# A recurrent mixer with its row modulation: the order of accumulations, gate products and the sum is changed, and rows and sums share one ring of buffers

## The chip, the core and the metric

The kernel runs on one core of a Trainium2 chip. The core has TensorE (matmuls, PE in the profile), VectorE (DVE), ScalarE (ACT), GpSimd (POOL) and SyncE (SP, whose queue issues the DMAs here). The metric is the device time of one execution in microseconds (us), the median of the runs.

## What is computed

One layer of a hybrid generator: a bidirectional gated linear recurrence (RG-LRU) over 256 context and 1024 latent tokens, with adaLN modulation, followed by a gated convolutional FFN. Cut to what the change touches:

```
sh1, sc1, g1, sh2, sc2, g2 = split((silu(c) @ mod_w + mod_b)[:, None, :], 6)   # rows of 1024
def lru_gates(xc, gate_w, gate_b, lam):                 # once for each direction
    pre = einsum("blhi,ghij->gblhj", xc.reshape(.., 10, 128), gate_w) + gate_b
    r, i = sigmoid(pre)
    log_a = -8 * softplus(-lam) * r
    return exp(log_a), sqrt(-expm1(2 * log_a)) * (i * xc)
def rglru_mixer(h, w_in, conv_w, conv_b, gates.., w_out):
    y, x = split(h @ w_in, 2)
    xc = dwconv1d(x, conv_w, conv_b)                    # 4 taps
    h_t = a_t * h_(t-1) + b_t                           # forwards and backwards
    return (gelu(y) * (h_fwd + h_bwd)) @ w_out
x = x + g1 * rglru_mixer(modulate(rms_norm(x), sh1, sc1))
x = x + g2 * conv_ffn(modulate(rms_norm(x), sh2, sc2))
```

## The kernel before

The 1280 channels of the recurrence are cut into ten blocks of 128, which lie across the partitions, with the 1280 tokens along the free dimension. Matrix products are made of three products of rounded parts: each operand is split into a high part (a cast on ScalarE, `S.copy`) and a low part (the difference, `lo_part`, on VectorE or GpSimd).

The loop `for t in range(NCH - 1)` (line 548) is what the text calls the passes, t = 0 to 8. In the code's own order, which the engines TensorE, VectorE, ScalarE and GpSimd keep, pass t does the following:

- TensorE runs the four gate products of block t (`gate(d, g)`, direction d, g = 0 for r and 1 for the input gate: three banks of 512, 512 and 256 tokens, nine matmuls), with the eight k steps of the next block's x product (`x_steps`) between them, then the two halves of the next block's y product (`y_half`). The gate products wait for `xs`, the split of the convolved x.
- ScalarE takes the sigmoids out of the banks (`gate_sig`), loads tables, makes the decays (`decay_a`, `decay_b`), the centre tap of the next convolution (`conv_centre`) and the casts.
- VectorE does the recurrence of the block before (`recur` for directions 0 and 1: r, b, then the scan), `gate_mul` for each input gate, the sum of both directions (`both`) and its product with the gelu (`gated`, which SP then stores), the other taps of the next convolution (`conv_taps`) and the low part of its split (`conv_split`).
- GpSimd makes the low parts of three weights in each pass: gate weights (`gwl`), and the x and y weights (`wl`).

Into this the kernel weaves the modulation rows g1, sh2, sc2, g2, eight halves of 512 columns. For each half, `mod_steps` has GpSimd clear an accumulator `macc` (one buffer), SP load the bias into its first row, and then eight times SP load 128 rows of the weight (`mraw`) and VectorE add them, scaled by silu(c), to `macc` (line 333). `mod(n)` takes n of these nine steps. When a half is full, `mod_hi` casts it to `mah`, `mod_lo` makes `mal`, `mod_sum` sums both over the partitions with a matmul against ones into a bank, and `mod_done` copies the bank to the row. The buffers of `mraw` are three, of `mah` and `mal` one each. The banks are five buffers of one pool (`bank()`); one that is asked for while all are taken waits for the reader of the one that comes free first.

Line 85 is `lo_part`, line 88 every matmul but the transposes (`mm`), line 439 `gate_mul`, lines 456 to 463 `recur`, 468 `both`, 472 `gated`, 405 `conv_taps`, 411 the casts of `conv_split`, 434 the sigmoids. SP's queue is not written by hand: its order is worked out when the program is built, and it is kept at run time.

Of the kernel before, what the change touches and what calls it, by code (L numbers as in the profile page):

```python
# [19 lines left out]
P = 128  # L20
# [22 lines left out]
XSPLIT = ((0, 512), (512, 1024), (1024, NTOK))  # L43
XLO_POOL = set()
HS_POOL = 0
MRAW = 3

GROUPS = tuple((j, j + 1) for j in range(0, NF, 2))
DOWN_LAST = {40: 3, 41: 1, 42: 2, 43: 3}
# [17 lines left out]
def tile_kernel(ctx: ExitStack, tc: tile.TileContext, x, cx, par, mod_b, mod1, mod2, wyx, gw, w_out, w_up, w_down, fw, out):  # L67
# [270 lines left out]
    def mod_hi():  # L338

        if not full:  # L340
            return None
        n, c, acc = full.pop(0)
        ah = mp.tile([P, 512], F32R, tag="mah", name="mah")
        al = mp.tile([P, 512], F32R, tag="mal", name="mal")
        S.copy(ah, acc)
        return n, c, acc, ah, al

    def mod_lo(m):
        if m:
            n, c, acc, ah, al = m  # L350
            lo_part(V, al, acc, ah)
# [10 lines left out]
    def mod_done(m):  # L362
        if not m:
            return
        n, c, pb = m
        dst = (g1, sh2, sc2, g2)[n]
        V.tensor_scalar(dst[:, c:c + 512], pb, float(n == 2), None, op0=ALU.add)
# [85 lines left out]
        return a  # L453

    def recur(d, a, r, b):
        V.scalar_tensor_tensor(r, a, 1.0, r, op0=ALU.add, op1=ALU.mult)  # L456
        V.tensor_tensor(b, b, r, op=ALU.mult)  # L457

        if d == 0:
            V.tensor_tensor_scan(a, a, b, 0.0, op0=ALU.mult, op1=ALU.add)  # L460
        else:
            V.tensor_tensor_scan(a[:, CTX - 1::-1], a[:, CTX - 1::-1], b[:, CTX - 1::-1], 0.0, op0=ALU.mult, op1=ALU.add)  # L462
            V.tensor_tensor_scan(a[:, NTOK - 1:CTX - 1:-1], a[:, NTOK - 1:CTX - 1:-1], b[:, NTOK - 1:CTX - 1:-1], a[:, 0:1], op0=ALU.mult, op1=ALU.add)  # L463
# [63 lines left out]
    with tc.manual_schedule(engines={ENG.PE, ENG.DVE, ENG.Activation, ENG.Pool}):  # L527
        xc = conv_centre(0, xp)
        wg = gate_weight(0)
        wx = weight(NCH + 1, G)  # L530
        conv_taps(0, xp, xc)
        xs = conv_split(xc)
        gy = y_done(y0)
        wy = weight(1, G)
        softplus_lambda()
        prev = None
        steps = mod_steps()

        def gate(d, g):
            bs = gate_mm(xs, wg, d, g)  # L540
            (r_t, b_t)[g][d] = dst = gate_sig(t, d, g, bs)
            return dst, bs

        def mod(n):
            for _ in range(n):
                next(steps, None)

        for t in range(NCH - 1):
            r_t, b_t = {}, {}
            xp, xo = x_outs()  # L550
            ks = iter(range(KD))

            def x_steps(n):
                for _ in range(n):
                    k_step(xo, CHUNKS, wx, next(ks))


            gate(0, 0)
            mh = mod_hi()
            x_steps(1)  # L560
            if prev:
                recur(0, prev[1][0], prev[2][0], prev[3][0])
            mod_lo(mh)
            i0 = gate(0, 1)
            if prev:
                recur(1, prev[1][1], prev[2][1], prev[3][1])
            gate_mul(*i0, xs[0])
            x_steps(2)
            pm = mod_sum(mh)
            mod(1)  # L570
            gate(1, 0)
            if prev:
                hs = both(prev[1], prev[2][1])
                gated(prev[0], hs, prev[4])
            mod_done(pm)
            x_steps(1)
            i1 = gate(1, 1)
            wg = gate_weight(t + 1)
            wx_next = weight(NCH + t + 2, G) if t < NCH - 2 else None
            mod(4)  # L580
            gate_mul(*i1, xs[0])
            x_steps(4)

            a_t = {d: wk.tile([P, NTOK], F32, tag="a", name="a", bufs=2) for d in range(2)}
            decay_a(t, 0, r_t[0], a_t[0])
            decay_b(t, 0, r_t[0])
            decay_a(t, 1, r_t[1], a_t[1])
            mod(4)
            xc = conv_centre(t + 1, xp)
            decay_b(t, 1, r_t[1])  # L590
            wy_next = weight(t + 2, G) if t < NCH - 2 else None
            conv_taps(t + 1, xp, xc)
            yb = [bank(), bank()]
            for q in range(2):
                y_half(yb, q, wy)
            wx, wy = wx_next, wy_next
            ordered(act(r_t[0], r_t[0], AF.Sqrt))
            xs = conv_split(xc)
            ordered(act(r_t[1], r_t[1], AF.Sqrt))
            prev = t, a_t, r_t, b_t, gy  # L600
            gy = y_done(yb)

        t = NCH - 1
        r_t, b_t = {}, {}
        gate(0, 0)
        recur(0, prev[1][0], prev[2][0], prev[3][0])
        i0 = gate(0, 1)
        gate_mul(*i0, xs[0])
        recur(1, prev[1][1], prev[2][1], prev[3][1])
        mh = mod_hi()  # L610
        mod_lo(mh)
        pm = mod_sum(mh)
        gate(1, 0)
        mod_done(pm)
        i1 = gate(1, 1)
        gate_mul(*i1, xs[0])
        hs = both(prev[1], prev[2][1])
        gated(prev[0], hs, prev[4])
        assert not full and next(steps, 0) == 0
# [290 lines left out]
```

## Time and profile before

| | us |
|---|---|
| median of 3 runs | 1323.93 |
| lowest and highest run | 1323.61, 1326.33 |
| the profiled execution | 1322.51 |
| its span, first to last instruction | 1320.7 |
| TensorE busy | 1243.8 (94%) |
| VectorE busy | 1052.8 (80%) |
| ScalarE busy | 548.7 (42%) |
| GpSimd busy | 426.3 (32%) |

A row of a timeline gives the start and the duration in us, the engine, the line, the operation, what it writes and reads with shapes, and how many equal ones are merged; in brackets stands the idle time ahead of it and what ended it. Matmuls are pipelined, so the distance between two starts tells more than a duration. A duration of VectorE or GpSimd holds what the instruction waited after it had begun.

### The profile page before, as it was taken

What the parts mean: (1) busy time and instruction counts of PE and PEld (TensorE: products, weight loads), DVE (VectorE), ACT (ScalarE), POOL (GpSimd) and SP (SyncE); (2) the same over time, 40 slices, a digit from 0 to 9 for tenths busy, and PEclk for the clock granted to TensorE, in tenths of its full rate; (3) what the DMA queues carried; (4) which work ended last, traced back from release to release, by engine and by line L of the source; (5) the groups of instructions that cost most, each with busy time, mean ns of one, the idle gap of its engine ahead of it and who ended that gap; (6) DMA issues with size and microseconds to landing.
All of it is one profiled execution on the core that took longest, in us unless ns stands there. A gap on an engine that the chain in (4) does not pass through costs nothing.

```text
span 1320.7 us, 14402 instructions
## 1 busy us (share of the span) xinstructions
PE 1243.8 (94%) x5512; PEld 1006.4 (76%) x5512; DVE 1052.8 (80%) x1193; ACT 548.7 (42%) x707; POOL 426.3 (32%) x238
## 2 busy tenths in 40 slices
PE   7789999898988889999999999999999999999995
PEld 6668777776767667878888888888888888888873
DVE  7968888888986877849977777777777777777788
ACT  6568776775777524433222222222222222222344
POOL 4632212111121300043143333333333333334565
PEclk8789999999998989999999999999999999999999
DMA  8413333332323464122111111111111111111003
GB/s 322 157 64 104 120 120 120 104 103 73 99 78 95 149 213 155 57 83 77 32 48 49 48 48 48 48 48 48 48 49 48 49 49 48 48 48 48 17 0 127
DMA packets 56740, 108.74 MB, mean 82 GB/s; under 512 B 4568, under 2 KB 24024, under 8 KB 56672
## 3 DMA queue, kind: packets, MB, share of 16 engines
q1 hardware_dynamic: 56528, 107.57, 24.5%
q8 instruction: 43, 0.70, 0.2%
q10 hardware_dynamic: 144, 0.26, 0.1%
q14 instruction: 25, 0.20, 0.0%
HBM read 98.37 MB, written 9.44 MB: 82 GB/s over the span
## 4 chain that ended last, share of the span: by engine, by line
PE 69%; DVE 18%; ACT 6%; DMA 3%; issue 3%; POOL 0%; SPq 0%; DVEq 0%; ACTq 0%
PE u L88 37%; PE pd L88 20%; PE pb L88 7%; PE xp L88 4%; DVE xc L405 3%; DMA mraw<-mod_dram 2%; DVE hl L213 2%; DVE a L463 2%; DVE macc L333 2%; DVE b L439 1%; DVE b L457 1%; DVE r L456 1%; DVE a L462 1%; ACT r L434 1%; DVE md L214 1%
## 5 line engine op out<-in xcount | busy, mean ns | idle before, releaser
L751 DVE SCALAR_TENSOR_TENSOR acc<-u,pr,acc 128x945 f32<-128x945 f32 (+2 forms) x352 | 427.0, 1219 | 23.3 <-ACT acc L744 15.9
L88 PE MATMUL u<-h2h,wl 128*128 128x512 f32 x704 | 277.7, 394 | 0.0
L88 PE MATMUL u<-h2l,wh 128*128 128x512 f32 x704 | 277.4, 394 | 0.0
L88 PE MATMUL u<-h2h,wh 128*128 128x512 f32 x704 | 274.4, 390 | 0.2 <-ACT h2h L717 0.2
L85 POOL TENSOR_TENSOR wl<-raw,wh 128x1024 fp32r<-128x1024 f32 x66 | 163.2, 2472 | 329.0 <-ACT wh L150 305.1
L784 DVE TENSOR_TENSOR x<-pd,x 128x512 f32<-128x512 f32 x160 | 109.6, 685 | 128.5 <-PE pd L88 128.5
L88 PEld LDWEIGHTS u<-h2l,wh 128*128 128x128 f32 x704 | 132.5, 188 | 31.7 <-DVE h2l L85 0.4
L88 PEld LDWEIGHTS u<-h2h,wh 128*128 128x128 f32 x704 | 132.5, 188 | 31.1 <-ACT h2h L717 0.5
L88 PEld LDWEIGHTS u<-h2h,wl 128*128 128x128 f32 x704 | 132.5, 188 | 28.1
L88 PE MATMUL pd<-dh,gl 128*128 128x512 f32 x320 | 126.3, 395 | 0.0
L88 PE MATMUL pd<-dl,gh 128*128 128x512 f32 x320 | 126.2, 394 | 0.0
L88 PE MATMUL pd<-dh,gh 128*128 128x512 f32 x320 | 125.2, 392 | 0.0
L830 ACT CAST gh<-acc 128x1024 fp32r<-128x1024 f32 x22 | 23.1, 1050 | 223.6 <-DVE acc L827 223.6
L85 POOL TENSOR_TENSOR gl<-acc,gh 128x1024 fp32r<-128x1024 f32 x18 | 43.2, 2400 | 199.0 <-ACT gh L830 199.0
L150 ACT CAST wh<-raw 128x1024 fp32r<-128x1024 f32 x64 | 67.2, 1050 | 79.4 <-PE u L88 73.4
L826 ACT ACTIVATE acc<-acc 128x1024 f32<-128x1024 f32 x22 | 23.3, 1060 | 182.8 <-DVE acc L751 182.8
L88 PE MATMUL xp<-hh,wh 128*128 128x512 f32 (+1 forms) x240 | 87.9, 378 | 1.9 <-ACT hh L223 1.9
L88 PE MATMUL xp<-hl,wh 128*128 128x512 f32 (+1 forms) x240 | 84.9, 378 | 4.0 <-POOL hl L85 4.0
L333 DVE SCALAR_TENSOR_TENSOR macc<-mraw,silu_c,macc 128x512 f32<-128x512 f32 x64 | 64.3, 1005 | 26.6 <-DMA mraw<-mod_dram 25.5
L88 PE MATMUL pb<-xh,gwh 128*128 128x512 f32 (+1 forms) x120 | 46.5, 387 | 27.1 <-DVE b L439 11.5
L88 PEld LDWEIGHTS pd<-dh,gl 128*128 128x128 f32 x320 | 60.0, 187 | 13.9
L88 PEld LDWEIGHTS pd<-dh,gh 128*128 128x128 f32 x320 | 60.1, 188 | 13.7
(188 smaller groups left out, 2306.6 us busy)
## 6 DMA issues: line engine op xcount, KB each, us to landing
raw<-w_up_dram SPq DMA_DIRECT2D x44, 512.0 KB, 3.6
mraw<-mod_dram SPq DMA_DIRECT2D x64, 256.0 KB, 3.5
raw<-wyx_dram SPq DMA_DIRECT2D x20, 512.0 KB, 3.5
dr<-w_down_dram SPq DMA_DIRECT2D x40, 256.0 KB, 3.8
ld<-mod_dram SPq DMA_DIRECT2D x16, 512.0 KB, 5.1
rgr<-rgd SPq DMA_DIRECT2D x16, 512.0 KB, 4.0
rgd<-r SPq DMA_DIRECT2D x10, 512.0 KB, 2.7
wor<-w_out_dram SPq DMA_DIRECT2D x10, 512.0 KB, 4.6
```

Source lines behind the costliest of these rows:

```text
L85: eng.tensor_tensor(lo, src, hi.bitcast(F32), op=ALU.subtract)
L88: T.matmul(o, w, r, start=start, stop=stop)
L150: S.copy(wh, raw)
L213: V.scalar_tensor_tensor(hl[KD - 1][:, :D], mr[k][s], 1.0, row, op0=ALU.mult, op1=ALU.mult, accum_out=md1[:, k, s, v:v + 1])
L214: V.tensor_scalar(md1[:, k, s], md1[:, k, s], mod_b1(k, s), None, op0=ALU.add)
L333: V.scalar_tensor_tensor(acc, r, silu_c[:, kk, 0:1], acc, op0=ALU.mult, op1=ALU.add)
L405: V.scalar_tensor_tensor(xc[:, oa:ob], xp[:, oa + s:ob + s], pr[:, C_CW + t * 4 + tap:C_CW + t * 4 + tap + 1], xc[:, oa:ob], op0=ALU.mult, ...
L463: V.tensor_tensor_scan(a[:, NTOK - 1:CTX - 1:-1], a[:, NTOK - 1:CTX - 1:-1], b[:, NTOK - 1:CTX - 1:-1], a[:, 0:1], op0=ALU.mult, op1=ALU.add)
L751: V.scalar_tensor_tensor(o, uv[:, r0 + dy:r1 + dy, c0 + dx:c1 + dx], w(dy, dx), o, op0=ALU.mult, op1=ALU.add)
L784: V.tensor_tensor(xs, pd, xs, op=ALU.add)
L826: ordered(act(aa, aa, AF.Silu))
L830: S.copy(gh, aa)
```

## The change

`mah` and `mal` are taken from the ring of `mraw` (tag "mraw"), which grows from three to five buffers. `recur` is cut into `recur_in` (r and b) and `recur_scan`. In the passes the second direction's scan moves behind the first `gate_mul`; one accumulation goes between the directions, two behind `gated`, four stay ahead of the taps and one goes between the taps and the split; the cast, low part, matmuls and copy of the sum move to later places of the pass. In the last block, t = 9, the calls for a sum, of which none is left there, are dropped.

```
-MRAW = 3
+MRAW = 5
...
-        ah = mp.tile([P, 512], F32R, tag="mah", name="mah")
-        al = mp.tile([P, 512], F32R, tag="mal", name="mal")
+        ah = mp.tile([P, 512], F32R, tag="mraw", name="mah", bufs=MRAW)
+        al = mp.tile([P, 512], F32R, tag="mraw", name="mal", bufs=MRAW)
...
     def recur(d, a, r, b):
+        recur_in(a, r, b)
+        recur_scan(d, a, b)
+
+    def recur_in(a, r, b):
         V.scalar_tensor_tensor(r, a, 1.0, r, op0=ALU.add, op1=ALU.mult)
         V.tensor_tensor(b, b, r, op=ALU.mult)
+
+    def recur_scan(d, a, b):
...
             gate(0, 0)
-            mh = mod_hi()
             x_steps(1)
             if prev:
-                recur(0, prev[1][0], prev[2][0], prev[3][0])
-            mod_lo(mh)
+                recur_in(prev[1][0], prev[2][0], prev[3][0])
+                recur_scan(0, prev[1][0], prev[3][0])
+                mod(1)
             i0 = gate(0, 1)
+            mh = mod_hi()
             if prev:
-                recur(1, prev[1][1], prev[2][1], prev[3][1])
+                recur_in(prev[1][1], prev[2][1], prev[3][1])
             gate_mul(*i0, xs[0])
             x_steps(2)
-            pm = mod_sum(mh)
-            mod(1)
             gate(1, 0)
+            if prev:
+                recur_scan(1, prev[1][1], prev[3][1])
+            mod_lo(mh)
             if prev:
                 hs = both(prev[1], prev[2][1])
                 gated(prev[0], hs, prev[4])
-            mod_done(pm)
             x_steps(1)
             i1 = gate(1, 1)
+            pm = mod_sum(mh)
+            mod(3)
             wg = gate_weight(t + 1)
             wx_next = weight(NCH + t + 2, G) if t < NCH - 2 else None
-            mod(4)
             gate_mul(*i1, xs[0])
+            mod_done(pm)
             x_steps(4)
...
             ordered(act(r_t[0], r_t[0], AF.Sqrt))
+            mod(1)
             xs = conv_split(xc)
...
-        mh = mod_hi()
-        mod_lo(mh)
-        pm = mod_sum(mh)
         gate(1, 0)
-        mod_done(pm)
         i1 = gate(1, 1)
```

What this does to VectorE's row of instructions in a pass, from the split of the convolution to the next taps. Before:

```order
L85 TENSOR_TENSOR mal<-macc,mah 128x512
L456 SCALAR_TENSOR_TENSOR r<-a,r 128x1280
L457 TENSOR_TENSOR b<-b,r 128x1280
L462 SCALAR_TENSOR_TENSOR a<-a,b 128x256
L463 SCALAR_TENSOR_TENSOR a<-a,b 128x1024
L439 TENSOR_TENSOR b<-pb,xc 128x512 x2
L439 TENSOR_TENSOR b<-pb,xc 128x256
L468 TENSOR_TENSOR r<-a 128x1024
L472 TENSOR_TENSOR r<-r,gy 128x1024
L367 TENSOR_SCALAR g_80<-pb 128x512
L333 SCALAR_TENSOR_TENSOR macc<-mraw,silu_c,macc 128x512 x4
```

VectorE now, the same stretch, from the accumulation that follows the scan of direction 0:

```order
L333 SCALAR_TENSOR_TENSOR macc<-mraw,silu_c,macc 128x512
L460 SCALAR_TENSOR_TENSOR r<-a,r 128x1280
L461 TENSOR_TENSOR b<-b,r 128x1280
L439 TENSOR_TENSOR b<-pb,xc 128x512 x2
L439 TENSOR_TENSOR b<-pb,xc 128x256
L468 SCALAR_TENSOR_TENSOR a<-a,b 128x256
L469 SCALAR_TENSOR_TENSOR a<-a,b 128x1024
L85 TENSOR_TENSOR mal<-macc,mah 128x512
L474 TENSOR_TENSOR r<-a 128x1024
L478 TENSOR_TENSOR r<-r,gy 128x1024
L333 SCALAR_TENSOR_TENSOR macc<-mraw,silu_c,macc 128x512 x2
```

The product b of the first input gate stands ahead of the two scans of direction 1, the low part of the sum behind them, and the accumulations are spread. (`a<-a,b` are the scans.)

On SP's queue the rows of a pass stood like this before, from the bias to the y weights (`DMAHW` are the DMA queues' own semaphores, the others name the engine that is waited for):

```order
L328 DMA macc<-mod_b_dram 1x512 [waits Pool_49]
L473 DMA rgd<-r 128x1024 [waits DVE_49]
L332 DMA mraw<-mod_dram 128x512 [waits DMAHW7_49,DMAHW5_49,DVE_49]
L332 DMA mraw<-mod_dram 128x512 [waits DMAHW0_49,DVE_49]
L332 DMA mraw<-mod_dram 128x512 [waits DMAHW1_49,DVE_49]
L156 DMA raw<-wyx_dram 128x1024 [waits Pool_49]
```

And on SP now:

```order
L328 DMA macc<-mod_b_dram 1x512 [waits Pool_49]
L332 DMA mraw<-mod_dram 128x512 [waits DMAHW5_49]
L479 DMA rgd<-r 128x1024 [waits DVE_49]
L332 DMA mraw<-mod_dram 128x512 [waits PE_49]
L332 DMA mraw<-mod_dram 128x512 [waits DMAHW6_49,DMAHW0_49,DVE_49]
L332 DMA mraw<-mod_dram 128x512 [waits DMAHW7_49,PE_49]
L156 DMA raw<-wyx_dram 128x1024 [waits Pool_49]
```

One row's load now stands ahead of the store of the gated product (`rgd<-r`), and two of the three behind it wait for TensorE, whose sum reads the buffers that they take.

## Rows read from the trace of the kernel before

**Rows 1.** The page's chain that ended last: share of the span by line.

```profile
PE u L88 37%; PE pd L88 20%; PE pb L88 7%; PE xp L88 4%; DVE xc L405 3%; DMA mraw<-mod_dram 2%; DVE hl L213 2%; DVE a L463 2%; DVE macc L333 2%; DVE b L439 1%; DVE b L457 1%; DVE r L456 1%; DVE a L462 1%; ACT r L434 1%; DVE md L214 1%
```

**Rows 2.** Busy time by pass (stretch, us, engines, PEclk, DMA): passes 1, 8, sum.

```profile
122.08:155.96 33.88, 33.10 (x160) 26.99 (x158) 28.45 (x31) 23.52 (x30) 7.64 (x4) 1.00 0.36 117
...
381.12:422.85 41.73, 37.47 (x159) 30.23 (x159) 30.49 (x31) 29.83 (x37) 7.05 (x3) 0.88 0.23 72
sum 300.77, PE 276.60 PEld 222.16 DVE 254.66 ACT 210.57 POOL 57.24; mean PE 34.58 PEld 27.77 DVE 31.83 ACT 26.32 POOL 7.15
```

**Rows 3.** Timeline of TensorE in pass 1: first matmuls of blocks.

```profile
130.86 0.39 PE L88 MATMUL pb<-mah,ones_r 128*128 128x512 f32 x1
...
131.32 0.39 PE L88 MATMUL pb<-xh,gwh 128*128 128x512 f32 x1
...
134.21 0.40 PE L88 MATMUL xp<-hh,wh 128*128 128x512 f32 x1
...
135.96 0.39 PE L88 MATMUL pb<-xh,gwh 128*128 128x512 f32 x1
...
137.69 0.40 PE L88 MATMUL xp<-hh,wh 128*128 128x512 f32 x1
```

**Rows 4.** Timeline of TensorE in pass 4: third bank of gate(1, 0).

```profile
245.78 0.38 PE L88 MATMUL pb<-xh,gwh 128*128 128x256 f32 x1 [1.78 <-DVE b L439]
```

**Rows 5.** Timeline of VectorE in pass 1.

```profile
119.98 1.48 DVE L456 SCALAR_TENSOR_TENSOR r<-a,r 128x1280 f32<-128x1280 f32 x1
...
123.03 2.82 DVE L460 TENSOR_TENSOR_SCAN a<-a,b 128x1280 f32<-128x1280 f32 x1
126.37 0.69 DVE L85 TENSOR_TENSOR mal<-macc,mah 128x512 fp32r<-128x512 f32 x1 [0.52 <-ACT mah L345]
...
130.03 0.69 DVE L462 TENSOR_TENSOR_SCAN a<-a,b 128x256 f32<-128x256 f32 x1
...
133.02 1.60 DVE L439 TENSOR_TENSOR b<-pb,xc 128x512 f32<-128x512 f32 x3
134.53 1.22 DVE L468 TENSOR_TENSOR r<-a 128x1024 f32<-128x1024 f32 x1
...
136.93 0.68 DVE L367 TENSOR_SCALAR g<-pb 128x512 f32<-128x512 f32 x1
137.53 2.32 DVE L333 SCALAR_TENSOR_TENSOR macc<-mraw,silu_c,macc 128x512 f32<-128x512 f32 x3
...
149.80 4.83 DVE L405 SCALAR_TENSOR_TENSOR xc<-xp,pr,xc 128x254 f32<-128x254 f32 x6
155.37 1.63 DVE L85 TENSOR_TENSOR xl<-xc,xh 128x512 fp32r<-128x512 f32 x3 [0.74 <-ACT xh L411]
```

**Rows 6.** Timelines of GpSimd and VectorE where the two meet.

```profile
106.57 2.87 POOL L85 TENSOR_TENSOR wl<-raw,wh 128x1024 fp32r<-128x1024 f32 x1
...
139.19 1.80 POOL L85 TENSOR_TENSOR gwl<-raw,gwh 128x512 fp32r<-128x512 f32 x1 [11.54 <-ACT gwh L381]
...
254.03 2.86 POOL L85 TENSOR_TENSOR wl<-raw,wh 128x1024 fp32r<-128x1024 f32 x1
...
391.47 3.33 POOL L85 TENSOR_TENSOR wol<-wor,woh 128x1024 fp32r<-128x1024 f32 x1 [16.39 <-ACT woh L482]
...
106.00 5.66 DVE L333 SCALAR_TENSOR_TENSOR macc<-mraw,silu_c,macc 128x512 f32<-128x512 f32 x4
...
254.54 1.61 DVE L439 TENSOR_TENSOR b<-pb,xc 128x512 f32<-128x512 f32 x3
```

**Rows 7.** SP's bias issue, DMA in 0.5 us behind it, landing of `mraw` loads.

```profile
200.57 0.24 SPq L328 DMA_DIRECT2D macc<-mod_b_dram  x1
...
201.00:201.50 0.50, 0.50 (x4) 0.45 (x3) 0.47 (x2) 0.00 (x0) 0.00 (x0) 1.00 0.03 4
...
DMA to landing us min/median/max: 2.7/3.5/3.7
```

**Rows 8.** Timeline of ScalarE in pass 1: the centre tap.

```profile
145.53 1.43 ACT L397 ACTIVATE xc<-xp,pr 128x1280 f32<-128x1280 f32 x1
```

## The prediction

> **What bounds the kernel now.** I read the chain of work that ended last first. It is TensorE's for the most part, but beside the matmuls it lists VectorE's accumulations of the row modulation (2% of the span) and the loads that these wait for (2% more) [rows 1]. Both belong to the mixer loop, so the second view is the busy table by pass of that loop, each stretch running from the first gate matmul of a pass to that of the next. Passes 1 to 8 take 300.77 us together, pass 1 33.88 and pass 8 41.73, with 160 and 159 matmul records; the granted clock is 1.00 in pass 1 and 0.88 in pass 8 [rows 2]. So matmul work does not set the time of a pass; waits do, and what the clock loses behind them.
>
> What would a pass take without waits? Pass 1 has one block that is too long: the gate block from 131.32 to 134.21 takes 2.89 where the next such block, 135.96 to 137.69, takes 1.73 [rows 3]. 33.88 less the 1.16 between them is **32.72 us**. Eight of these are 261.8, so some 39.0 us lie in these passes for any change of this kind.
>
> Whom TensorE waits for is seen in pass 4: 1.78 us for the product b of VectorE [rows 4], because the third bank of gate(1, 0) is freed by `gate_mul` of the first gate, and that stands behind both scans of direction 1.
>
> **The change, step by step.** Every pass keeps its matmuls, its eight accumulations, its GpSimd operations and its bytes. What moves is the order on VectorE, TensorE's sum and SP's queue, and with them the waits. I lay out pass 1 anew in the printed times: TensorE begins at 122.08 (the start of the stretch in [rows 2]), VectorE at 119.98, 2.10 us ahead [rows 5].
>
> *TensorE.* The two sum matmuls (0.46, 130.86 to 131.32 [rows 3]) move behind gate(1, 1). Without them and without the wait the block of gate(1, 1) begins 1.62 earlier, at 134.34, and the pass ends at 122.08 + 32.72 = 154.80.
>
> *VectorE*, by the distances between starts in [rows 5]; a step's successor begins 0.09 before the printed end (133.02 + 1.60 against 134.53), so an accumulation, three of which take 2.32, counts about 0.76 in a row and 0.67 alone. r and b of direction 0, 3.05, and its scan, 2.82: 125.85. The moved accumulation, 0.67: 126.52; the wait of 0.52 for the cast of the sum, which stood here, is gone. r and b of direction 1, 3.05: 129.57. `gate_mul`, 1.51: 131.08. Its first third is over by 130.1, and TensorE comes to that bank at 134.34 - 1.75 - 0.35 = 132.2 (one x step and a third of a block earlier), so a wait as in pass 4 is covered by 2 us. The scans of direction 1, 2.99: 134.07. The low part of the sum, 0.69 less that 0.09, 0.60: 134.67; TensorE reads it at 134.34 + 1.73 = 136.07, so the new wait in front of its x matmuls is covered by 1.4. The sum of the directions and its product, 2.40: 137.07. Then two accumulations (1.45), the second `gate_mul` (1.5), the sum's copy (0.60), four accumulations (3.03), taps with the 0.74 behind them (5.57) and the split (1.55). The last accumulation stands in those 0.74, in which VectorE waits for ScalarE's cast anyway, so 0.67 costs nothing; without that cover it would cost 0.67 a pass. All of it: 3.05 + 2.82 + 0.67 + 3.05 + 1.51 + 2.99 + 0.60 + 2.40 + 1.45 + 1.5 + 0.60 + 3.03 + 5.57 + 1.55 = 30.8 us without waits.
>
> *GpSimd* brings the waits. The low part of the gate weights is asked for 3.23 after the block of gate(1, 1) begins (135.96 [rows 3] to 139.19 [rows 6]), now at 137.57. That is inside the first accumulation (137.07 to about 137.8). How the two engines collide is seen at 106.57: a GpSimd operation that came during the first of four accumulations ran next, and the four took 5.66 instead of 3.1 [rows 6]. So the second accumulation waits out the gate weights, 1.3 us, and the third waits for what is left of the next operation, 2.4 us. Between these two accumulations lie the product and the copy, 2.1 us, which read PSUM; a product at 254.54 took its usual 1.61 in the middle of a GpSimd operation that began at 254.03 [rows 6]. So 0.3 is left. Bounds: nothing if GpSimd comes after both accumulations, 1.3 + 2.4 = 3.7 if it comes before 137.07. I take 1.6, the case of the layout, whose margin is 0.5 us. VectorE's pass is then 32.4 against TensorE's 32.72, so its lead and that margin grow from pass to pass.
>
> *Loads.* Two of five buffers' uses in each turn are now the sum's parts. So two of the rows for the four accumulations wait for TensorE's sum, and all three that are not yet loaded stand on SP's queue behind the store of the gated product, which waits until 137.07. SP issues them at about 137.5 to 138.5; a row lands 2.7 to 3.7 later [rows 7], by 142.2. VectorE wants the last at 144.6: covered by 2.4. The next weights, behind these on SP, have ten us to spare. The new start of a sum also waits for its bias row: GpSimd clears the sum behind the low part (I set 0.6 for its 512 columns, as VectorE's copy of as many takes), then SP issues. In pass 3 this was at 200.57 and the row moved before 201.50 [rows 7]; with the same again for its semaphore I take 1.1 us. 134.67 + 0.6 + 1.1 = 136.4, ahead of 137.07. Bounds: that, and the 3.7 of a whole row, 1.9 a pass late. The Trainium skill's page "DMA: Bandwidth & Descriptors", section "Anatomy of one DMA", gives about 2.0 us of fixed cost per transfer for its GpSimd path; this load goes by SP and the trace shows less, and by the page it would land at 137.3 and cost an estimated 0.2 a pass.
>
> *ScalarE.* The centre tap began 6.34 after the gate weights were asked for (139.19 to 145.53 [rows 6, 8]); so now at 143.9, ending at 145.3, where VectorE's accumulations end at 145.4. No wait.
>
> Passes 1 to 7 take 32.72. *Pass 8* has one accumulation left, and a GpSimd operation for the output weights, which takes 3.33 today [rows 6]. Its cast now stands ahead of the first sigmoids, so it meets the first scan: VectorE is 2.4 late, and its lead hides half. I take 1.2 (bounds 0 and 3.3): 33.9.
>
> Sum: 7 x 32.72 + 33.9 = 262.9 against 300.77, **37.9 us saved**. What follows is TensorE's matmuls as before and shifts along. The profiled execution took 1322.51, so 1284.6; the median of the runs lies 1.42 above it: **1286 us**.
>
> **The rivals.** *GpSimd takes its whole price (B).* If its operation comes 0.5 earlier against VectorE, the product and the next accumulation wait 1.3 and 2.4, VectorE's pass is 30.8 + 3.7 = 34.5, its lead is gone, TensorE then follows it through `gate_mul`, and every further pass is alike. Pass 1 at 33, six at 34.5, pass 8 at 36: 276, saved 24.8, 1299; if it starts only later in the loop, between 1286 and 1299. For it: the margin is small. Against it: VectorE's pass is the shorter one without it. The Trainium skill's page "SBUF — State Buffer", section "SBUF: two separate sides", says that VectorE operations with two SBUF inputs and GpSimd take one port pair as an exclusive lock, and that the loser blocks for the whole instruction. By that rule accumulations put beside GpSimd's work are paid in full, which is this rival's 34.5; the trace agrees that they block (5.66 for 3.1).
>
> *A third collision (C).* If in B the four accumulations run later still, the low part of the y weights, which meets the taps otherwise (they read PSUM), meets them, 2.4 more: six passes at 36.9, with 33 and 36: 290, saved 10.4, 1314. For it: that low part follows the centre tap closely, and the tap ends where the accumulations end. Against it: a late VectorE delays the centre tap as well, since the tap's buffer is read by the second `gate_mul`.
>
> *The loads become the wait (D, the slower one).* The last three rows are issued only behind the gated product. They are wanted 6 us after that. Each us beyond holds seven passes, so all is given back from 6 + 37.9/7 = 11.4 us to landing; at 12.5 it is 1331. The longest landing is 3.7 [rows 7].
>
> *The wait only changes its name (E).* If ScalarE's sigmoids hold TensorE wherever VectorE did, nothing is saved: 1324.
>
> **How the numbers follow.** Forecast 0.50; B, whole or from a later pass, 0.34; C 0.08; D 0.04; E 0.04. The range 1281 to 1304 holds the first two (0.84): B is up to 5 us worse if pass 8 and the bias row are at their upper bounds too, and the low end is eight passes at 32.72 (1285) less some us of the last pass, whose wait I don't price. Faster by over 0.2% (about what a measurement here can tell from no change) 0.92, within it 0.04, slower 0.04.
>
> **What the profile will show.** Passes 1 to 7 at 32.7, clock 1.00, no wait for b: right. Passes of 34 to 35 with the gated product or an accumulation drawn out by 1.3 and 2.4 beside GpSimd: B. Accumulations that wait for loads: D. Waits for r at the gates in each pass: E. I am wrong at the root if the loop shrinks and the total does not.

## The result and the profile after

| | before | changed |
|---|---|---|
| median (us) | 1324.49 | 1284.08 |
| lowest and highest of 4 runs | 1323.61, 1326.33 | 1282.26, 1291.12 |
| the profiled execution | 1322.51 | 1282.26 |
| its span | 1320.7 | 1280.5 |
| TensorE busy | 1243.8 (94%) | 1227.7 (96%) |
| VectorE busy | 1052.8 (80%) | 1045.2 (82%) |

The changed kernel takes 0.9703 of the time before (95% interval 0.9665 to 0.9741), 40.4 us less. In the profiled executions the span is 40.2 shorter: 39.31 of it in passes 1 to 8, 0.34 ahead of them (the loop's pass 1 begins at 121.74 where it began at 122.08), and 0.55 behind them (1280.5 - 383.20 against 1320.7 - 422.85). The 0.34 and 0.55 are no more than executions of one kernel differ by: in another execution of the changed kernel ("changed, again" below) the passes take 261.46 as well, but begin at 123.45. One of the four runs took 1291.12; four more runs of the same kernel lie between 1283.24 and 1284.86.

The busy table by pass answers to [rows 2]. Columns: stretch, its length, then busy time and count for TensorE, its weight loads, VectorE, ScalarE, GpSimd, the granted clock, DMA share and GB/s.

```profile
121.74:154.40 32.66, 32.66 (x159) 27.14 (x158) 31.64 (x35) 26.77 (x33) 7.06 (x4) 1.00 0.36 122
...
317.70:350.36 32.66, 32.66 (x159) 27.14 (x158) 31.54 (x35) 26.57 (x32) 6.95 (x4) 1.00 0.33 106
350.36:383.20 32.84, 32.84 (x160) 27.13 (x159) 26.97 (x28) 26.18 (x32) 8.58 (x3) 1.00 0.29 91
sum 261.46, PE 261.46 PEld 217.07 DVE 247.87 ACT 212.43 POOL 57.40; mean PE 32.68 PEld 27.13 DVE 30.98 ACT 26.55 POOL 7.17
```

TensorE is busy for the whole of each pass: 32.66 of 32.66, seven times over, and 261.46 of 261.46 in all. The clock is 1.00 throughout, where pass 8 had 0.88. No row of TensorE in these passes has a wait of its own left, neither for b [rows 4] nor for r.

VectorE in pass 1, and GpSimd beside it, answer to [rows 5, 6]:

```profile
125.46 0.73 DVE L333 SCALAR_TENSOR_TENSOR macc<-mraw,silu_c,macc 128x512 f32<-128x512 f32 x1
...
129.03 1.61 DVE L439 TENSOR_TENSOR b<-pb,xc 128x512 f32<-128x512 f32 x3
130.56 0.68 DVE L468 TENSOR_TENSOR_SCAN a<-a,b 128x256 f32<-128x256 f32 x1
...
133.54 0.67 DVE L85 TENSOR_TENSOR mal<-macc,mah 128x512 fp32r<-128x512 f32 x1
...
136.52 2.54 DVE L333 SCALAR_TENSOR_TENSOR macc<-mraw,silu_c,macc 128x512 f32<-128x512 f32 x2
138.99 1.60 DVE L439 TENSOR_TENSOR b<-pb,xc 128x512 f32<-128x512 f32 x3
140.51 0.67 DVE L367 TENSOR_SCALAR g<-pb 128x512 f32<-128x512 f32 x1
141.11 3.15 DVE L333 SCALAR_TENSOR_TENSOR macc<-mraw,silu_c,macc 128x512 f32<-128x512 f32 x4
144.86 4.83 DVE L405 SCALAR_TENSOR_TENSOR xc<-xp,pr,xc 128x254 f32<-128x254 f32 x6 [0.60 <-ACT xc L397]
149.61 0.74 DVE L333 SCALAR_TENSOR_TENSOR macc<-mraw,silu_c,macc 128x512 f32<-128x512 f32 x1
...
137.21 1.30 POOL L85 TENSOR_TENSOR gwl<-raw,gwh 128x512 fp32r<-128x512 f32 x1 [2.42 <-ACT gwh L381]
138.46 2.87 POOL L85 TENSOR_TENSOR wl<-raw,wh 128x1024 fp32r<-128x1024 f32 x1
```

GpSimd's request comes at 137.21, 0.69 behind the start of the first accumulation. The two accumulations take 2.54; the same two took 1.53 in pass 6, where the request came a little later. So the collision costs 1.0 here. The product at 138.99 takes its usual 1.60 beside GpSimd. In passes 2 to 7 the request comes 1.0 behind the first accumulation, and the collision moves to the group of four behind the product, which loses 1.3 there. Pass 2, VectorE:

```profile
172.41 4.39 DVE L333 SCALAR_TENSOR_TENSOR macc<-mraw,silu_c,macc 128x512 f32<-128x512 f32 x4
```

Two rows of the waits by engine and line, of all eight passes (who waits for whom, us in total, times, longest), of the changed kernel:

```profile
DVE xc L405 <- ACT xc L397: 8.7, 8, 5.0
DVE macc L333 <- DMA mraw<-mod_dram: 1.2, 3, 0.5
```

And the same view of the kernel before, in a row that the prediction did not show:

```profile
DVE macc L333 <- DMA mraw<-mod_dram: 24.2, 19, 2.4
```

The accumulations' waits for loads fell from 24.2 us to 1.2. A row lands later than before (median 4.4 after issue against 3.5), yet it is there when it is wanted.

### The profile page after: what moved, and what is told of

Read it like the earlier page. It is cut to its first block, busy times and chain, and to the rows that moved or that the text cites. A ratio compares the mean times of both kernels' runs of the same rounds, so it can differ in the third digit from the quotient of the medians.

```text
span 1280.5 us, 14366 instructions
## 1 busy us (share of the span) xinstructions
PE 1227.7 (96%) x5512; PEld 1000.2 (78%) x5512; DVE 1045.2 (82%) x1193; ACT 550.6 (43%) x707; POOL 426.6 (33%) x238
## 4 chain that ended last, share of the span: by engine, by line
PE 83%; DVE 11%; ACT 3%; issue 2%; DMA 1%; POOL 0%; SPq 0%; DVEq 0%; ACTq 0%
PE u L88 38%; PE pd L88 20%; PE pb L88 14%; PE xp L88 10%; DVE hl L213 2%; DVE xc L405 1%; DVE md L214 1%; DVE stat L112 1%; DMA ld<-x_dram 1%; DVE rgl L85 1%; PE pt L720 0%; DVE x L790 0%; DVE b L461 0%; PE pb L270 0%; DVE o L860 0%
## 5 line engine op out<-in xcount | busy, mean ns | idle before, releaser
L88 PE MATMUL xp<-hh,wh 128*128 128x512 f32 (+1 forms) x240 | 84.9, 366 | 1.8 <-ACT hh L223 1.8
L88 PE MATMUL xp<-hl,wh 128*128 128x512 f32 (+1 forms) x240 | 82.0, 366 | 4.4 <-POOL hl L85 3.7
L88 PEld LDWEIGHTS pd<-dh,gh 128*128 128x128 f32 x320 | 60.1, 188 | 13.7
L88 PEld LDWEIGHTS pd<-dl,gh 128*128 128x128 f32 x320 | 60.0, 187 | 13.6
L769 POOL TENSOR_TENSOR dr<-dr,g 128x512 f32<-128x512 f32 x40 | 52.0, 1318 | 53.8 <-DMA dr<-w_down_dram 53.8
```

The source lines that it names most:

```text
L88: T.matmul(o, w, r, start=start, stop=stop)
L769: G.tensor_tensor(raw, raw, g2[:, cs], op=ALU.mult)
```

## The experiments

The passes now stand at TensorE's own time. What the runs had to settle is which part brings this, and whether the margins were as the prediction put them. Three theories were set against each other. **Turn**: a pass lasts the longer of TensorE's 32.66 and VectorE's own turn, and a VectorE that comes late meets GpSimd and becomes later still. **Product**: TensorE's waits for b, and the clock lost behind them, are the matter, so the early product brings the gain. **Loads**: the 24.2 us are the matter, so the ring brings it.

| kernel | eight passes | median | ratio to before (95%) |
|---|---|---|---|
| before | 300.77 | 1324.49 | 1 |
| changed | 261.46 | 1284.08 | 0.9703 (0.9665 to 0.9741) |
| ring alone | 274.47 | 1296.36 | 0.9794 (0.9755 to 0.9832) |
| product alone | 306.55 | 1329.34 | 1.0045 (1.0027 to 1.0064) |
| ring and product | 274.42 | 1298.04 | 0.9821 (0.9804 to 0.9837) |
| changed, no ring | 289.75 | 1313.66 | 0.9924 (0.9895 to 0.9953) |
| changed, product late | 271.29 | 1294.03 | 0.9768 (0.9732 to 0.9805) |
| changed, accumulations together | 275.11 | 1297.28 | 0.9826 (0.9796 to 0.9857) |
| changed, three accumulations early | 276.27 | 1298.60 | 0.9832 (0.9801 to 0.9863) |
| changed, four buffers | 261.48 | 1283.44 | 0.9720 (0.9683 to 0.9757) |
| changed, sum early | 261.55 | 1283.80 | 0.9724 (0.9694 to 0.9753) |
| changed, last block reordered | 261.46 | 1282.93 | 0.9707 (0.9690 to 0.9724) |
| changed, again | 261.46 | 1283.87 | 0.9715 (0.9699 to 0.9730) |

Each ratio is to runs of the kernel before that were taken with it (medians 1320.67 to 1324.49), so medians of different rows compare to a few us only; the eight passes of the profiled executions compare better.

**The ring alone**, on the kernel before:

```
-MRAW = 3
+MRAW = 5
...
-        ah = mp.tile([P, 512], F32R, tag="mah", name="mah")
-        al = mp.tile([P, 512], F32R, tag="mal", name="mal")
+        ah = mp.tile([P, 512], F32R, tag="mraw", name="mah", bufs=MRAW)
+        al = mp.tile([P, 512], F32R, tag="mraw", name="mal", bufs=MRAW)
```

> The kernel before with one part of the change: rows and sums share five buffers; every other order as before. Three theories. Turn: a pass lasts as long as the longer of TensorE's 32.66 and VectorE's own turn, which in the kernel before was lengthened by waits for loads (24.2 us in the eight passes), by the wait for the sum's cast (0.5 a pass) and by GpSimd's collisions. Then the ring takes away the 3.0 of loads a pass, and the turn is 30.8 + 0.67 (the accumulation that is not hidden) + 0.5 + some 2.2 of collisions = 34.2: eight passes 274, time about 1297 (1293 to 1305). Loads: the 24.2 us are the whole matter, so the ring alone brings nearly all: below 1290. Product: the waits of 1.78 and 3.26 for b, and the clock lost behind them, are the matter; the ring leaves them: 1315 or more, and waits for b in passes 2, 4, 6, 8 as before.

Measured: 1296.36, the turn theory's number, but not by its mechanism. Seven passes are alike at 33.80 to 33.88, the only wait of TensorE in pass 3 is 0.78 for r, and each pass has one like it. VectorE is not what it waits for: its two groups of four accumulations lose 0.9 and 0.6 to GpSimd (4.02 and 3.74 for 3.1). The timelines of TensorE, ScalarE and VectorE in pass 3:

```profile
189.59:223.47 33.88, 33.10 (x159) 27.00 (x158) 32.24 (x35) 26.42 (x33) 7.56 (x4) 1.00 0.36 117
...
198.37 0.40 PE L88 MATMUL pb<-mah,ones_r 128*128 128x512 f32 x1
...
200.46 0.50 PE L88 MATMUL pb<-xh,gwh 128*128 128x512 f32 x1 [0.78 <-ACT r L434]
...
199.72 0.69 ACT L434 ACTIVATE r<-pb,pr 128x512 f32<-128x512 f32 x1 [3.92 <-PE pb L88]
...
200.53 1.59 DVE L439 TENSOR_TENSOR b<-pb,xc 128x512 f32<-128x512 f32 x3
205.03 4.02 DVE L333 SCALAR_TENSOR_TENSOR macc<-mraw,silu_c,macc 128x512 f32<-128x512 f32 x4
```

The second bank of gate(1, 0) begins at 200.46, right behind the sigmoid of that gate's own first bank (199.72 + 0.69). It has to take that bank again: the three of gate(0, 1) are held until the product, which begins at 200.53, and the sum holds the fifth. This is the block of 2.89 of [rows 3], which the prediction took out as a stall. The kernel before has this wait for r in all eight passes; in pass 1 it is TensorE's only one:

```profile
132.94 0.50 PE L88 MATMUL pb<-xh,gwh 128*128 128x512 f32 x1 [0.78 <-ACT r L434]
```

**The product alone**, on the kernel before (with `recur` cut in two as in the change):

```
-                recur(1, prev[1][1], prev[2][1], prev[3][1])
+                recur_in(prev[1][1], prev[2][1], prev[3][1])
             gate_mul(*i0, xs[0])
+            if prev:
+                recur_scan(1, prev[1][1], prev[3][1])
```

> The kernel before with one part of the change: the first gate's product ahead of the second direction's scan; buffers and accumulations as before. Turn: the waits for b go, but VectorE's turn keeps its waits for loads (3.0 a pass), 0.5 for the cast and about 1 to 2 of collisions: 30.8 + 0.67 + 0.5 + 3.0 + 1.3 = 36.3, so eight passes take about 288 to 292 and the time is about 1312 (1306 to 1318); TensorE then waits for the split of x at the start of the passes. Product: nearly the whole gain comes from here: 1295 or less, passes of 33 to 34. Loads: nothing is gained, 1324.

Measured: 1329.34, slower than before (0.45%, its interval clear of no change), which no theory expected. TensorE's waits for b are gone, but it waits for the split of x at the start of the passes (2.71 at 198.36), and every pass from the second on is like the long ones of before, 38.8 to 39.9 (the last 36.8). Pass 3 of it, by pass and by timeline:

```profile
198.36:237.31 38.95, 34.96 (x159) 28.15 (x159) 35.02 (x35) 26.26 (x33) 7.70 (x4) 0.94 0.32 102
...
217.36 6.04 DVE L333 SCALAR_TENSOR_TENSOR macc<-mraw,silu_c,macc 128x512 f32<-128x512 f32 x4
...
228.24 0.75 DVE L333 SCALAR_TENSOR_TENSOR macc<-mraw,silu_c,macc 128x512 f32<-128x512 f32 x1 [1.21 <-DMA mraw<-mod_dram]
229.54 2.27 DVE L333 SCALAR_TENSOR_TENSOR macc<-mraw,silu_c,macc 128x512 f32<-128x512 f32 x1 [0.55 <-DMA mraw<-mod_dram]
...
217.43 1.82 POOL L85 TENSOR_TENSOR gwl<-raw,gwh 128x512 fp32r<-128x512 f32 x1 [9.96 <-ACT gwh L381]
...
228.72 2.54 POOL L85 TENSOR_TENSOR wl<-raw,wh 128x1024 fp32r<-128x1024 f32 x1 [6.65 <-PE pb L88]
```

GpSimd's request at 217.43 falls on the first accumulation (217.36), and the four take 6.04, 3.0 more than without. Then the loads are waited for, and so the last accumulation meets the low part of the y weights (2.27 for 0.75). TensorE, no longer held by b, reaches its gates sooner, so ScalarE's cast and GpSimd's request come sooner against VectorE; the wait for b had kept them apart in every other pass. That last sentence is read from the timelines, not tested by a run of its own. The wait of 0.78 for r at gate(1, 0) is here too (at 211.24), since the product, early in the order, begins only at 209.73 and ends after TensorE has come to the second bank.

**The changed kernel without the ring** (three buffers for the rows, `mah` and `mal` one each; the first diff reversed):

> The changed kernel without the shared ring: three buffers for the rows, one each for the sum's two parts, as before; every order as changed. Turn: the four accumulations in a row wait for loads again, 2 to 3 a pass; VectorE's turn 32.4 less the 0.6 in which it waits for the centre tap, plus 2.5 to 3 = 34.5: passes 1 to 7 about 1.9 longer each, 1297 (1291 to 1303). Product: nothing lost, 1284. Loads: the 24.2 come back whole, 1306 or more.

Measured: 1313.66, later than the turn theory had it. Pass 1 takes 32.66, then the passes grow: 35.26, 35.77, and from pass 4 on 37.2 to 37.5 (the last 36.8). Pass 5:

```profile
282.49 4.61 DVE L333 SCALAR_TENSOR_TENSOR macc<-mraw,silu_c,macc 128x512 f32<-128x512 f32 x2
...
293.36 2.73 DVE L333 SCALAR_TENSOR_TENSOR macc<-mraw,silu_c,macc 128x512 f32<-128x512 f32 x1 [1.90 <-DMA mraw<-mod_dram]
...
282.09 1.63 POOL L85 TENSOR_TENSOR gwl<-raw,gwh 128x512 fp32r<-128x512 f32 x1 [1.33 <-ACT gwh L381]
...
293.14 2.40 POOL L85 TENSOR_TENSOR wl<-raw,wh 128x1024 fp32r<-128x1024 f32 x1 [6.60 <-ACT wh L150]
```

One load is waited for, 1.90. But a VectorE that is late by that much is met by GpSimd at 282.09, ahead of its two accumulations (4.61 instead of 1.53), and the accumulation behind the load is met by the y weights (2.73 instead of 0.75). 1.9 us of wait bring 5 us of collisions. My expectation held the first and left the second out.

**The changed kernel with the product late:**

```
                 recur_in(prev[1][1], prev[2][1], prev[3][1])
+                recur_scan(1, prev[1][1], prev[3][1])
             gate_mul(*i0, xs[0])
             x_steps(2)
             gate(1, 0)
-            if prev:
-                recur_scan(1, prev[1][1], prev[3][1])
             mod_lo(mh)
```

> The changed kernel with the first gate's product behind the second direction's scan again, as before; all else as changed. Turn: TensorE comes to the third bank of gate(1, 0) at 131.9 in pass 1, and the product's first third is done near 133; from that matmul round to itself (12.95 to the end of the centre tap, 7.2 to the next r, 9.36 + 2.99 + 0.55 to the first third of the product) it is 33.0 instead of 32.66, so a pass costs about 0.4 more and the first about 1: time about 1287 (1285 to 1291), with a wait for b in each pass. Product: the waits for b come back with their clock: 1305 or more. Loads: 1284, no difference.

Measured: 1294.03, with a wait for b in each pass as expected, but 7 us more than expected. Two of these rows of TensorE (passes 3 and 8), VectorE at the taps of pass 3, and VectorE in pass 8:

```profile
200.10 0.39 PE L88 MATMUL pb<-xh,gwh 128*128 128x256 f32 x1 [0.46 <-DVE b L439]
...
369.30 0.39 PE L88 MATMUL pb<-xh,gwh 128*128 128x256 f32 x1 [2.57 <-DVE b L439]
...
213.19 4.83 DVE L405 SCALAR_TENSOR_TENSOR xc<-xp,pr,xc 128x254 f32<-128x254 f32 x6 [1.07 <-ACT xc L397]
...
359.80 2.83 DVE L333 SCALAR_TENSOR_TENSOR macc<-mraw,silu_c,macc 128x512 f32<-128x512 f32 x1
```

Passes 2 to 7 take 33.4 to 33.5; pass 3, with its listed wait of 0.46, takes 33.39, 0.7 above 32.66. VectorE is not late in these passes, since it waits 1.07 for the centre tap: the pass is as long as the way from the product over TensorE, the tap and the recurrence back to the product, as the expectation had it (33.0 there). Pass 8 takes 37.04, 4.2 more than in the changed kernel: there the accumulation meets GpSimd's output weights (2.83), the scans follow, and the late product passes this on to TensorE. The early product swallows the same collision.

**The changed kernel with the accumulations together** (in two groups of four):

```
                 recur_scan(0, prev[1][0], prev[3][0])
-                mod(1)
...
-            mod(3)
+            mod(5)
...
             ordered(act(r_t[0], r_t[0], AF.Sqrt))
-            mod(1)
```

> The changed kernel with the accumulations in two groups of four again, behind the gated product and ahead of the taps, as before; ring, product and sum as changed. Turn: VectorE's turn is 30.8 + 0.67 (the last accumulation is not hidden). The four behind the gated product begin 0.64 earlier, at about 135.9, so the third and the fourth meet GpSimd's two operations (1.3 and 2.4): the taps begin 2.7 later than in the changed kernel, which uses up VectorE's lead of 2.1 in one pass. A late VectorE then pays 3.7, and more where the y weights' low part meets the second group: turns of 35 to 37 from the third pass on, as the last passes of the kernel without the ring show (37.2). Time about 1302 (1294 to 1316). If spreading the accumulations is worth nothing beside the ring, the product and the sum: 1284 to 1287.

**The same with three accumulations early:**

```
                 recur_scan(0, prev[1][0], prev[3][0])
-                mod(1)
+                mod(3)
...
-            mod(4)
+            mod(3)
...
             ordered(act(r_t[0], r_t[0], AF.Sqrt))
-            mod(1)
```

> The changed kernel with two accumulations moved ahead: three behind the scan of direction 0, two behind the gated product, three ahead of the taps, none hidden. The work is the same, but the gated product ends 1.45 later, at 138, behind GpSimd's request at 137.2. If the margin decides, as rival B has it: GpSimd's two operations cost 3.7 (or the 2.4 of the second at least), VectorE's lead of 2.1 goes in the first passes, and the turn is then 30.8 + 0.67 + 3.7 = 35.2 and up to 37: time about 1304 (1296 to 1316), with the first pass at 32.7. If it does not decide: the turn is 30.8 + 0.67 + 1.1 = 32.6, passes of 32.7, time 1284.

Measured: 1297.28 and 1298.60, as the turn theory had it. With three early, pass 1 is 32.67 and then six passes take 34.4 to 34.6. Pass 3 of the kernel with three early, VectorE and GpSimd:

```profile
191.02:225.55 34.53, 33.30 (x159) 27.07 (x158) 33.44 (x35) 26.48 (x33) 7.62 (x4) 1.00 0.36 114
...
208.06 2.25 DVE L478 TENSOR_TENSOR r<-r,gy 128x1024 f32<-128x1024 f32 x1
210.23 3.69 DVE L333 SCALAR_TENSOR_TENSOR macc<-mraw,silu_c,macc 128x512 f32<-128x512 f32 x2
...
207.93 1.30 POOL L85 TENSOR_TENSOR gwl<-raw,gwh 128x512 fp32r<-128x512 f32 x1 [0.45 <-ACT gwh L381]
209.18 3.40 POOL L85 TENSOR_TENSOR wl<-raw,wh 128x1024 fp32r<-128x1024 f32 x1
```

And the group of four in pass 3 of the kernel with the accumulations together, 3.0 longer than the four of the changed kernel's pass 1 (passes of 34.5 to 34.9 from the third on, a little below the turns expected):

```profile
205.23 6.17 DVE L333 SCALAR_TENSOR_TENSOR macc<-mraw,silu_c,macc 128x512 f32<-128x512 f32 x4
```

The gated product is drawn out from 1.22 to 2.25 and the two accumulations from 1.53 to 3.69, 3.2 together. This is rival B, with its place and its signs; a turn of 34.5 and a time of 1299 were written down for it. The turn has other parts than B's, though: the collisions cost 3.2, not 3.7, and one accumulation is no longer hidden (0.67), so 30.8 + 0.67 + 3.2 = 34.7. What B asks for, a request ahead of the first accumulation, is given in pass 1 already (139.39 against 140.28), and there the two accumulations take 4.61, as they do in the kernel without the ring, where the request is 0.4 ahead.

**The changed kernel with four buffers** (`MRAW = 4`):

> The changed kernel with four buffers in the ring instead of five, so that each load starts one use later: this takes cover from the loads (rival D's cause). By the layout the second to last row is asked for at 138.9, lands 4.4 later at 143.3, and is wanted at 143.4; the last is freed at 142.5 and wanted at 149.6. VectorE waits 0.6 for the centre tap anyhow, so little is lost: 1284 to 1290. If the cover is as thin as that and VectorE comes late, it meets GpSimd and the passes go to 37 as without the ring: 1300 or more.

Measured: 1283.44, every pass as with five. VectorE's waits for loads come back in part and are all covered:

```profile
DVE macc L333 <- DMA mraw<-mod_dram: 8.9, 12, 1.4
```

**The changed kernel with the sum early**, at its old place ahead of gate(1, 0):

```
             gate(0, 0)
+            mh = mod_hi()
...
-                mod(1)
+            mod_lo(mh)
             i0 = gate(0, 1)
-            mh = mod_hi()
...
             x_steps(2)
+            pm = mod_sum(mh)
             gate(1, 0)
...
-            mod_lo(mh)
...
             i1 = gate(1, 1)
-            pm = mod_sum(mh)
             mod(3)
...
-            mod(1)
+            mod(2)
             xs = conv_split(xc)
```

> The changed kernel with the sum at its old place on TensorE, ahead of gate(1, 0) (its cast and low part earlier too; the eighth accumulation with the seventh ahead of the split); ring, product and the other accumulations as changed. The kernel with the ring alone has passes of 33.86, 1.2 above 32.66, with a wait of 0.78 for r at the second bank of gate(1, 0): the sum holds the fifth bank, so that bank must be the first one again, behind its sigmoid. If that is so, the wait comes back whole here, though VectorE is on time: passes of 33.8 to 33.9, pass 8 without a wait for b at about 34, time about 1293 (1291 to 1296). If the 1.2 belongs to VectorE's order instead: 1284, no wait for r.

Measured: 1283.80, no wait for r: the expectation fell. Passes of 32.7, as pass 3, with the first product on VectorE and the gate's second bank on TensorE:

```profile
187.78:220.47 32.69, 32.69 (x159) 27.13 (x158) 31.66 (x35) 26.34 (x33) 6.94 (x4) 1.00 0.36 122
...
195.65 1.61 DVE L439 TENSOR_TENSOR b<-pb,xc 128x512 f32<-128x512 f32 x3
...
197.69 0.39 PE L88 MATMUL pb<-xh,gwh 128*128 128x512 f32 x1
```

The product, at 195.65, is through (197.26) before the gate's second bank at 197.69, so three banks are free by then and the sum's place does not matter. What held the bank in the kernel with the ring alone was the late product together with the sum; taking away the product's lateness is enough.

**Ring and product**, on the kernel before (the first two diffs together):

> The kernel before with two parts of the change: the shared ring of five and the first gate's product ahead of the second scan; the sum and the accumulations as before. If the parts add up: the ring alone gives passes of 33.86 with a wait of 0.78 for r, and the early product takes that wait away whatever the sum's place (the kernel with the sum early shows 32.69), so passes are 32.7 and the time 1284. Turn and GpSimd: with the accumulations in two groups of four, VectorE's turn is 31.5 + 0.5 for the sum's cast + at least 1.6 of collisions (0.95 and 0.7 in the kernel with the ring alone) = 33.6, longer than TensorE's 32.7; so its lead goes, it meets GpSimd in full (3.1 as in the kernel with the accumulations together) and the turn becomes about 35: eight passes about 278, time 1300 (1295 to 1306), no better than the ring alone.

Measured: 1298.04, passes of 34.6 to 34.7 from the third on. The parts do not add up: on top of the ring the early product is worth 0.05 us in eight passes, as long as the accumulations stand in two groups. In pass 3 GpSimd's request comes 0.7 ahead of the first group (208.10 against 208.82), where with the ring alone it came 1.7 behind it (206.70 against 205.03). The group behind the gated product of that pass (four without a collision take 3.1):

```profile
190.14:224.77 34.63, 33.53 (x160) 26.94 (x158) 33.03 (x35) 26.37 (x33) 7.10 (x4) 1.00 0.36 117
...
208.82 5.59 DVE L333 SCALAR_TENSOR_TENSOR macc<-mraw,silu_c,macc 128x512 f32<-128x512 f32 x4
```

**Beyond the loop.** With the passes at TensorE's time, the next place to look is the last block, t = 9, where a low part stands ahead of the directions' sum and GpSimd collides again. One try to go past the changed kernel held the casts and low parts of the second to fourth operand back behind that sum; it ran beside the changed kernel itself.

```
-        hi(gh[:, :NCH - 2], raw)
+        ins = hi(gh[:, :NCH - 2], raw)
+        if after:
+            tc.add_manual_dep(ins.ins, after, NOSYNC, reason="keep the recurrence first")
...
-    rg_first += [rg_part(i, 0, V.tensor_copy) for i in range(1, 4)]
+    rg_first += [rg_part(i, 0, V.tensor_copy, b8) for i in range(1, 4)]
```

`b8` names the sum of both directions of block 8.

> The changed kernel, and in the last block (t = 9) the casts and low parts of the out projection's second to fourth operand held back until the sum of both directions of the block before. In the changed kernel they stand ahead of that sum on VectorE and, with GpSimd's low parts beside them, delay it by about 7.8 us (0.6 + 2.8 + 1.1 + 3.3), and ScalarE's decays wait for it for 4.5. If that chain (sum, decays, last recurrence) sets the end of the block, 4 to 6 us come back: about 1279. If TensorE then lacks those operands as much as it gains, nothing changes: 1284; it waits some 5 us for the second operand.

> The changed kernel itself, beside the kernel with the last block reordered, to compare the two on one chip: 1284 (1281 to 1287), eight passes of 261.5.

Measured: 1282.93 beside 1283.87, ratios of 0.9707 (0.9690 to 0.9724) and 0.9715 (0.9699 to 0.9730): no difference that these runs can tell. The sum does come earlier, at 400.06 instead of 407.59, but the last recurrence begins as before (417.54 and 417.53): VectorE now waits ahead of it for the load of an operand. TensorE's waits between 383 and 440 us have moved but not shrunk (12.2 us against 12.1 in "changed, again"). One row of VectorE and one of TensorE:

```profile
415.46 0.70 DVE L504 CAST rgh<-rgr 128x1024 fp32r<-128x1024 f32 x1 [4.75 <-DMA rgr<-rgd]
...
408.90 0.80 PE L88 MATMUL pb<-woh,rgl 128*128 128x512 f32 x1 [3.63 <-DVE rgl L85]
```

## Why the prediction was right, and where it was not

**The time and the pass.** 1286 was forecast, 1284.08 measured. Passes 1 to 7 are 32.66 where 32.72 was laid out from [rows 2, 3]; the stall was read as 1.16 and was worth 1.2.

**VectorE's layout.** Step by step it holds to about 0.2 us: the product was laid out at 129.57 and began at 129.03, the scans 131.08 and 130.56, the low part 134.07 and 133.54, the first accumulation 137.07 and 136.52. 0.31 of each difference is VectorE's earlier start. The waits that it declared covered (the bank, the low part of the sum, the bias row) are not there; the bias row is issued at 134.82, and the first accumulation begins 1.70 later without a listed wait.

**GpSimd.** 1.6 us a pass was taken; 1.1 was measured in pass 1 and 1.3 in passes 2 to 7. In pass 1 the request at 137.21 fell into the end of the first accumulation, as laid out, the second waited 1.0 instead of 1.3, and the group of four lost about 0.1 instead of 0.3. Rival B is real, as the kernel with three accumulations early shows, but its margin was 0.7, not 0.5, its collisions cost 3.2, not 3.7, and its price of 34.5 was met there only because 0.67 of an unhidden accumulation came on top. No run shifts VectorE by just 0.7; the one there is shifts it by 1.45.

**The centre tap.** "No wait" was wrong by a little: VectorE waits 0.60 for it in pass 1. It makes up for what GpSimd costs less, so that the turn of 32.4 (32.32 in pass 1) came out right by two errors that cancel, which is luck. It also means that VectorE's lead over TensorE does not grow from pass to pass, as the prediction said it would: it is 2.1 at the start of pass 1 (119.67 against 121.74), 2.4 at the start of pass 2 (151.99 against 154.40) and still 2.4 at that of pass 7 (315.29 against 317.70), since ScalarE's tap follows TensorE and VectorE is held to it.

**Pass 8.** 33.9 was forecast, 32.84 measured. The collision is there (the accumulation at 353.73 took 2.84), but VectorE has no accumulation after it in that pass and waits 5.0 for the centre tap, so nothing of it reaches TensorE. The term should have been 0.1, not 1.2; the difference of 1.5 in the loop is the 1.1 from here and seven times 0.06. The prediction set VectorE's lead against the collision and left out the cover of 2 us that it had itself given the early product; with the product late the same collision does reach TensorE (pass 8 at 37.04).

**What was misread: the cause.** The prediction began with TensorE's wait for b [rows 4] and, after naming the loads' 2% of the chain [rows 1], treated them as a risk alone (rival D). The stall of pass 1 that it took out is not even a wait for b, but one for r. The runs say otherwise. The early product alone makes the kernel slower by 0.45%. The ring alone brings 26.3 of the 39.3 us; the clock is back at 1.00 in seven of its eight passes, and no run tells how much of the 26.3 is the clock's. The prediction's sum was right because its layout let every accumulation go without a wait, which is the ring's doing; it never said so, nor gave the 24.2 us of waits for loads that the trace of before holds. Taken away from the finished change, the ring costs 28.3 us, the spread of the accumulations 13.7, the early product 9.8, the sum's new place 0.1. These add up to more than 39.3, since what one part is worth depends on the others. Without the ring or the spread VectorE falls behind, meets GpSimd, and the passes settle at 37 or 34.5. With the product late VectorE is in time, but TensorE waits for b, and the passes settle at 33.4. Only with all three does TensorE wait for nothing.

**The rivals.** B did not come, but stands 0.7 us away in pass 1 and 1.0 in the later ones. C shows in the kernel without the ring, at 37.2 to 37.5 a pass against the 36.9 laid out, with a load's wait in it. D is far off: even four buffers suffice, though three, with separate ones for the sum, do not. E did not come, and its sign was a poor one: waits for r stand in every pass of the kernel before. At gate(1, 0) they belong to a product that ends too late for TensorE, by its place (ring alone) or because VectorE is late (product alone).

## What to carry to other kernels

Lay the engines' turns side by side before believing a wait's name: TensorE's wait for b was where a late VectorE showed, not what made it late. Where two engines lock each other out, place the requests of one beside operations that don't collide (here those that read PSUM), and price every delay with the collisions that it brings: 1.9 us of waiting cost 5 more. Test the parts of such a change both ways, alone and taken away, since one that is needed at the end can be worth nothing, or less, by itself.

## What the hardware showed

A VectorE cast with one SBUF operand is held by GpSimd as well. Two casts of the same shape in the last block of the changed kernel, and GpSimd beside the second:

```profile
386.97 0.67 DVE L501 CAST rgh<-rgr 128x1024 fp32r<-128x1024 f32 x1
...
393.82 2.86 DVE L501 CAST rgh<-rgr 128x1024 fp32r<-128x1024 f32 x1
...
393.72 5.19 POOL L85 TENSOR_TENSOR wol<-wor,woh 128x1024 fp32r<-128x1024 f32 x2 [18.52 <-ACT woh L488]
```

0.67 alone, 2.86 beside GpSimd. The Trainium skill's page "SBUF — State Buffer", section "SBUF: two separate sides", counts VectorE operations in a two-port performance mode among those that take the lock, beside those with two SBUF inputs; the rows agree that it is held, and I had reckoned with the second kind alone. The trace names no mode; the cast takes 0.67 for 1024 columns, where an addition of two inputs of as many takes 1.22 (134.12).

When both engines have work queued they take turns, one operation each: in the kernel with three accumulations early the gated product ran between GpSimd's two operations and lengthened the second (3.40 where it takes 2.4 alone), and the accumulations behind it waited in their turn.

A short wait of TensorE costs more than its row lists: 0.46 for b cost 0.7 in its pass, 0.78 for r 1.2, at a granted clock of 1.00 in both passes. Why is not shown.
